# One PSUM pool, a fourth plain column tile, and a written order for pooling and attention in a two-layer trunk

## The chip, the cores and the metric

One core of a Trainium2 chip runs the whole model. The engines are TensorE (PE; its weight loads are listed as PEld), VectorE (DVE), ScalarE (ACT), GpSimd (POOL) and SyncE (SP). Time is device microseconds (us) of one execution; the kernel before took 1059.41 us as the median of 3 runs (1058.34 to 1059.82).

## The reference

A residual stream of 528 tokens (16 learned meta tokens, then 512) by 1024 features passes two layers and a final RMSNorm. Layer 0 mixes tokens by causal pooling, layer 1 by stick-breaking attention with 16 heads of 64; each is followed by a SwiGLU FFN with 2816 hidden features.

```python
h = concat(meta, x)                                       # (528, 1024)
h = h + pool_mixer(rmsnorm(h), pool_w, pool_scale)        # windows 2, 4, 8, 16
h = h + (silu(n @ w_gate[0]) * (n @ w_up[0])) @ w_down[0] # n = rmsnorm(h)
h = h + sb_attention(rmsnorm(h), w_qkv) @ w_o
h = h + (silu(n @ w_gate[1]) * (n @ w_up[1])) @ w_down[1]
out = rmsnorm(h)[16:]
# attention: z = q k / 8; a = exp(log_sigmoid(z) + sum over later allowed keys of log_sigmoid(-z)); o = a v
```

## The kernel before, in words

**Numbers.** Every operand of a large matmul is split into a high part (fp32r, by ACT: `whi`, `uh`, `hh`, `xh`) and the rest (by DVE: `wlo`, `ul`, `hl`, `xl`), and a product is three matmuls (high x high, high x low, low x high; `mm3`, L102). Weights come by DMA on SP's queue into a ring of 6 raw tiles and are split into rings of 8 (`wsplit`, L82; NW). Tiles of 128 x 528 share a ring of 29 (`blk`).

**FFN** (`ffn`, L269–476). The hidden features are 22 column tiles f of 128. The first PLAIN = 3 of them are made plainly: gate and up, 8 chunks of depth each (`plain`, L353). The others by one step of Strassen's scheme on pairs (`strassen`, L392): token halves, depth halves and the gate/up pair make seven products pa, pb, pc in place of eight. It needs sums of the weights (`sums`, L400) and of the normalised input (`operands`, L373: seven arrays `xh[i]`, `xl[i]` of 4 chunks, made once a layer in four rounds m of two chunks). The plain tiles use the input without the norm's factor and multiply by it after the product; so the norm's sum over features (a matmul with ones, `norm_bcast`, names `fb0`, `fb1`) is issued after the first gate product. ROUNDS cuts the 22 tiles into rounds; while a round's tiles are made, the previous round is multiplied by w_down (`down` in layer 0, over 264 tokens; `down_n` in layer 1, with tokens on partitions and 512 features, tiles `pd`).

**PSUM** has 8 banks. `phase` opens a pool for each part: the start with 8 single banks, FFN 0 with w = 6 and d = 2, attention with 4 single and 2 double tiles, FFN 1 with 6 and 2. A pool's banks are given to the next pool when everything in the old one is read.

**Start.** Pooling is matmuls of tokens (`ah`, `al`) with band matrices, two token halves for 8 chunks, scaled into `ph`, `pl`; then `mix`, per half and chunk, is added to the stream `hT`, and `norm.chunk` splits a chunk and sums its squares.

**Attention** (L486–723, in 8 pairs p of heads). For a pair: projections `pj` of q, k, v in five steps, scores `z` in three groups, sigmoids on ACT, a reverse scan on DVE (`kp`) and a product (`sg`), transposes `t`, products with v (`po`), and `wo`, the output projection of pairs 0–1, 2–4 and 5–7 (tiles `pw0_c`, `pw2_c`, `pw5_c` for chunk c), the first two of them placed between the pairs' steps.

**End.** In layer 1's last round each 128-token block t is finished by `square` (sum of squares on ACT) and `store` (factor, scaling, DMA out).

**Order.** A scheduler orders each engine's instructions by a simulated timeline; `tc.issue_after(x)` keeps what stands in it behind instruction x. The names' suffix in the profile leaves tile numbers out: pp is every plain product.

Of the kernel before, what the change touches and what calls it, by code (L numbers as in the profile page):

```python
# [13 lines left out]
P = 128  # L14
# [16 lines left out]
PLAIN = 3  # L31
# [19 lines left out]
def trunk(ctx: ExitStack, tc: tile.TileContext, x, meta, x_t, gain, pool_w, w_qkv, w_o, w_gate, w_up, w_down,  # L51
# [11 lines left out]
    @contextmanager  # L63
    def phase(name, **bufs):
        with tc.tile_pool(name=name, bufs=1, space=bass.MemoryType.PSUM) as pool:
            psum["pool"], psum["bufs"] = pool, bufs
            yield
# [33 lines left out]

    def mm3(outs, wh, wl, xh, xl, start, stop, more=False):  # L102

        for i, (w, xx) in enumerate(((wh, xh), (wh, xl), (wl, xh))):
            for o, sl in outs:
                last = nc.tensor.matmul(o, lhsT=w, rhs=xx[:, sl], start=start and i == 0, stop=stop and i == 2,  # L106
                                        skip_group_check=more)
        return last.ins
# [17 lines left out]
    def add_eps(out, sq, acc):  # L126

        nc.vector.scalar_tensor_tensor(out, sq, D * EPS / P, acc, op0=ALU.add, op1=ALU.add)

    last_rstd = []  # L130
# [11 lines left out]
    class Norm:  # L142
# [5 lines left out]
        def chunk(self, c):  # L148
# [9 lines left out]
            if c == KC - 1:  # L158
                add_eps(self.acc, sq, self.acc)
# [5 lines left out]
    def norm_bcast(accs, name, tag):  # L165
# [4 lines left out]
        for o in range(0, w, h):  # L170
            p = ps(f"{name}p{o}", tag)[:, :h]
            for i, acc in enumerate(accs):
                nc.tensor.matmul(p, lhsT=ones, rhs=acc[:, o:o + h], start=i == 0, stop=i == len(accs) - 1)
# [6 lines left out]
    with tc.tile_pool(name="start", bufs=1) as sp, phase("ps0", one=8):  # L180
# [52 lines left out]
        pw = ps("warm", "one")  # L233
# [3 lines left out]
        ph, pl = [], []  # L237
        for c in range(KC):
            for dst, n in ((ph, "ph"), (pl, "pl")):
                dst.append(blk(f"{n}{c}", F32R) if c < 6 else sp.tile([P, L], F32R, name=f"{n}{c}"))  # L240
        for hf, terms in enumerate((((0, -META), (1, -144)), ((1, 120), (2, HALF - 272), (3, -136)))):
            for c in range(KC):
                g = c // 2
                cs = slice(c * P, (c + 1) * P)
                pp = ps(f"pool{c}{hf}", "one")[:, :HALF]
                for j, (i, off) in enumerate(terms):
                    rhs = band[:, g, BOFF + off:BOFF + off + HALF]
                    nc.tensor.matmul(pp, lhsT=ah[i][:, cs], rhs=rhs, start=j == 0, stop=False)
                    nc.tensor.matmul(pp, lhsT=al[i][:, cs], rhs=rhs, start=False, stop=j == len(terms) - 1)
                    if hf == 0 and j == 0:  # L250
                        nc.tensor.matmul(pp[:, 0:32], lhsT=am[:, cs], rhs=mband[:, g, :], start=False, stop=False)
# [5 lines left out]
        for hf in range(2):  # L257
            for c in range(KC):
                g, d = c // 2, c % 2
                pm = ps(f"mix{c}{hf}", "one")[:, :HALF]  # L260
                for k in range(2):
                    ds = slice(d * P, (d + 1) * P)
                    mm3([(pm, HV[hf])], pws[k][0][g][:, ds], pws[k][1][g][:, ds], ph[2 * g + k], pl[2 * g + k],
                        k == 0, k == 1)
# [6 lines left out]
    def ffn(layer, gcol, norm, after):  # L271
# [48 lines left out]
        def down_n(r, t, e, hid, w, tag="d", sl=slice(0, 512)):  # L320
# [8 lines left out]
            for j, (wh, wl) in enumerate(zip(*w)):  # L329
                for i, (x_, w_) in enumerate(((0, wh), (1, wh), (0, wl))):  # L330
                    nc.tensor.matmul(pd, lhsT=hid[j][x_][:, ts], rhs=w_[:, sl], start=r > 0 and i + j == 0,  # L331
                                     stop=j == len(hid) - 1 and i == 2, skip_group_check=r == 0)
# [3 lines left out]
            else:  # L336
                nc.vector.tensor_tensor(out=hv, in0=pd, in1=hv, op=ALU.add)

        with tc.tile_pool(name=f"ffn{layer}", bufs=1) as fp:

            def wk(name):
                return fp.tile([P, HALF], F32, tag="wk", name=name, bufs=8)[:, :n]

            def gw(name):
                return fp.tile([P, L], F32, tag="gw", name=name, bufs=4)[:, :nt]
# [7 lines left out]
            def plain(f):  # L353
                parts = [wsplit(raw_gu(kind, f), f"w{kind}{f}") for kind in ("gate", "up")]
                g, sg, u = (gw(f"{i}{f}") for i in ("g", "sg", "u"))
                for dst, (wh, wl) in zip((g, u), parts):
# [444 lines left out]
```

## Time and profile before

| | |
|---|---|
| median of 3 runs | 1059.41 us (1058.34 to 1059.82) |
| the profiled execution | 1062.8 us |
| its span | 1061.0 us |
| granted PE clock, mean | 0.985 |
| PE busy | 1023.1 us, 96% |
| DVE busy | 856.6 us, 81% |
| ACT busy | 556.9 us, 52% |
| moved by DMA | 95.73 MB, mean 90 GB/s |

The span is cut here into the start (0 to 52), FFN 0 (52 to 403), attention (403 to 691) and FFN 1 (691 to 1061). A busy PE is the time in which its array is at work, at whatever clock the throttle granted; a stage with PE busy throughout and the clock at 1.00 runs at its cadence. The profile's rows give the time an instruction took alone; a run of equal ones is denser, since they overlap.

### The profile page before, as it was taken

Reading aid. Unit: us, or ns where it says so; the run is one execution under the profiler, and the core shown is the slowest. Engines: PE = TensorE matmul, PEld = TensorE weight load, DVE = VectorE, ACT = ScalarE, POOL = GpSimd, SP = SyncE. Lnnn points to the kernel's source line nnn. Section 1 sums busy time; section 2 is a strip of 40 time slices with the busy share of each in tenths; the row PEclk is TensorE's granted clock in tenths of the full one; section 3 lists DMA queues with packets and bytes.
Section 4 is the critical chain, followed back from the end, with each engine's and each line's share of the span. In section 5 each row is a group of like instructions: output and inputs, shape, how many; then the busy total and the mean of one; then the engine's idle time right before and its main releaser. Section 6 shows DMA issues by size and latency. Waiting matters only on the chain.

```text
span 1061.0 us, 18586 instructions
## 1 busy us (share of the span) xinstructions
PE 1023.1 (96%) x7302; PEld 949.3 (89%) x7302; DVE 856.6 (81%) x1529; ACT 556.9 (52%) x1131; POOL 6.2 (1%) x16
## 2 busy tenths in 40 slices
PE   8998999999999999999999998989999999999997
PEld 6997999999999998998888886867899999999985
DVE  7899987888878777678888987779977877788755
ACT  7555645454444455455555454555655444455544
POOL 1000000000000010000000000000000000000000
PEclk9999999999999999999999998989999999999999
DMA  9212323333333332211111211211223223333302
GB/s 351 72 51 69 128 94 100 101 100 100 100 100 100 99 120 82 78 40 61 40 51 37 69 58 66 80 62 58 100 100 115 84 100 99 100 100 120 109 31 80
DMA packets 43112, 95.73 MB, mean 90 GB/s; under 512 B 3328, under 2 KB 20096, under 8 KB 43024
## 3 DMA queue, kind: packets, MB, share of 16 engines
q1 hardware_dynamic: 42272, 93.40, 26.2%
q8 instruction: 57, 0.93, 0.3%
q10 hardware_dynamic: 752, 1.14, 0.3%
q14 instruction: 31, 0.25, 0.1%
HBM read 92.43 MB, written 2.10 MB: 89 GB/s over the span
## 4 chain that ended last, share of the span: by engine, by line
PE 78%; DVE 17%; issue 2%; ACT 1%; DMA 1%; SPq 0%; ACTq 0%; DVEq 0%
PE pb L106 15%; PE pd L106 11%; PE pd L331 11%; PE pa L106 10%; PE pc L106 10%; PE pj L106 9%; PE pp L106 4%; DVE kp L581 2%; PE pw L106 2%; PE z L567 2%; DVE xl L390 1%; DVE a L619 1%; PE t L594 1%; DVE t L387 1%; DVE sg L583 1%
## 5 line engine op out<-in xcount | busy, mean ns | idle before, releaser
L304 DVE TENSOR_TENSOR h<-pd,h 128x264 f32<-128x264 f32 x96 | 40.9, 427 | 14.0 <-PE pd L106 14.0
L92 ACT CAST ws_3h<-rgate 128x512 fp32r<-128x512 f32 x38 | 23.6, 620 | 53.3 <-PE pb L106 47.8
L581 DVE TENSOR_TENSOR_SCAN kp<-kp,estrip 128x1344 f32<-128x1344 f32 x16 | 47.3, 2954 | 3.8 <-ACT kp L576 3.4
L92 ACT CAST ws_4h<-s 128x512 fp32r<-128x512 f32 x38 | 23.6, 621 | 46.6 <-PE pa L106 27.7
L92 ACT CAST ws_5h<-s 128x512 fp32r<-128x512 f32 x38 | 23.6, 621 | 45.8 <-PE pb L106 34.7
L433 DVE TENSOR_TENSOR u<-pb,m 128x264 f32<-128x264 f32 (+1 forms) x38 | 16.3, 428 | 38.6 <-PE pb L106 38.6
L106 PE MATMUL pa<-xl,ws_0h 128*128 128x264 f32 (+1 forms) x152 | 43.3, 285 | 3.1 <-DVE xl L390 3.0
L106 PE MATMUL pb<-xl,ws_1h 128*128 128x264 f32 (+1 forms) x152 | 43.3, 285 | 1.0 <-DVE xl L390 1.0
L106 PE MATMUL pc<-xl,ws_2h 128*128 128x264 f32 (+1 forms) x152 | 43.1, 283 | 0.9 <-DVE xl L390 0.9
L106 PE MATMUL pb<-xh,ws_1h 128*128 128x264 f32 (+1 forms) x152 | 43.6, 287 | 0.2 <-ACT xh L389 0.2
L106 PE MATMUL pa<-xh,ws_3h 128*128 128x264 f32 (+1 forms) x152 | 43.6, 287 | 0.0
L106 PE MATMUL pa<-xl,ws_3h 128*128 128x264 f32 (+1 forms) x152 | 43.5, 286 | 0.0
L106 PE MATMUL pa<-xh,ws_3l 128*128 128x264 f32 (+1 forms) x152 | 43.3, 285 | 0.0
L106 PE MATMUL pc<-xh,ws_2l 128*128 128x264 f32 (+1 forms) x152 | 43.2, 284 | 0.0
L106 PE MATMUL pa<-xh,ws_0h 128*128 128x264 f32 (+1 forms) x152 | 43.1, 284 | 0.0
L106 PE MATMUL pb<-xh,ws_6l 128*128 128x264 f32 (+1 forms) x152 | 43.0, 283 | 0.0
L106 PE MATMUL pa<-xh,ws_0l 128*128 128x264 f32 (+1 forms) x152 | 43.0, 283 | 0.0
L106 PE MATMUL pb<-xh,ws_4l 128*128 128x264 f32 (+1 forms) x152 | 43.0, 283 | 0.0
L106 PE MATMUL pc<-xl,ws_5h 128*128 128x264 f32 (+1 forms) x152 | 42.9, 283 | 0.0
L106 PE MATMUL pb<-xh,ws_1l 128*128 128x264 f32 (+1 forms) x152 | 42.9, 283 | 0.0
L106 PE MATMUL pb<-xl,ws_4h 128*128 128x264 f32 (+1 forms) x152 | 42.9, 282 | 0.0
L106 PE MATMUL pc<-xh,ws_5h 128*128 128x264 f32 (+1 forms) x152 | 42.9, 282 | 0.0
(1179 smaller groups left out, 4110.9 us busy)
## 6 DMA issues: line engine op xcount, KB each, us to landing
rgate<-in_ffn_w_gate_dram SPq DMA_DIRECT2D x44, 512.0 KB, 3.5
rup<-in_ffn_w_up_dram SPq DMA_DIRECT2D x44, 512.0 KB, 3.5
rd<-in_ffn_w_down_dram SPq DMA_DIRECT2D x42, 512.0 KB, 3.6
rq<-in_sb_w_qkv_dram SPq DMA_DIRECT2D x8, 512.0 KB, 3.5
rk<-in_sb_w_qkv_dram SPq DMA_DIRECT2D x8, 512.0 KB, 3.4
rv<-in_sb_w_qkv_dram SPq DMA_DIRECT2D x8, 512.0 KB, 3.4
rwo<-in_sb_w_o_dram SPq DMA_DIRECT2D x8, 384.0 KB, 3.0
h<-in_x_t_dram SPq DMA_DIRECT2D x8, 264.0 KB, 6.9
```

Of the source, the lines that this page charges most:

```text
L92: nc.scalar.copy(hi, v[:, j:j + w])
L106: last = nc.tensor.matmul(o, lhsT=w, rhs=xx[:, sl], start=start and i == 0, stop=stop and i == 2, skip_group_check=more)
L304: nc.vector.tensor_tensor(out=hv, in0=pd, in1=hv, op=ALU.add)
L331: nc.tensor.matmul(pd, lhsT=hid[j][x_][:, ts], rhs=w_[:, sl], start=r > 0 and i + j == 0, stop=j == len(hid) - 1 and i == 2, skip_group_ch ...
L387: nc.vector.tensor_tensor(out=o, in0=a, in1=b, op=ALU.subtract)
L390: nc.vector.tensor_tensor(out=xl[i][:, m, :], in0=o, in1=f32(xh[i][:, m, :]), op=ALU.subtract)
L433: tt(out=u[:, a], in0=pb, in1=m1, op=ALU.add)
L567: nc.tensor.matmul(tz[:, hd, c:c + k1 - k0], lhsT=qq[hs, i * P:(i + 1) * P], rhs=kk[hs, k0:k1], start=j == 0 and c == 0, stop=False, skip_ ...
L581: nc.vector.tensor_tensor_scan(kp[:, hd, ::-1], kp[:, hd, ::-1], estrip[:, ::-1], 1.0, op0=ALU.mult, op1=ALU.max)
L583: return nc.vector.tensor_tensor(out=sg[:, hd, 0:STRIP - 1], in0=sg[:, hd, 0:STRIP - 1], in1=kp[:, hd, 1:STRIP], op=ALU.mult).ins
L594: nc.tensor.transpose(o, sg[:, c0:c0 + n], ident)
L619: nc.vector.scalar_tensor_tensor(a0[r, i], f32(a0h[r]), lo_rows[r], p2[r, 256:384], op0=ALU.mult, op1=ALU.add)
```

## The change

- PLAIN is 4: tile f = 3 of each layer is made plainly.
- One PSUM pool for the whole program, with tags `two` (2 tiles of two banks), `c` and `d` (2 of one bank each). `one` takes c and d in turn, `any` in the start goes round all eight banks, `ps_pair` gives a plain tile's two accumulators as a two-bank tile or as two of c. Strassen's pa and pb share a two-bank tile, `pab`.
- Pooling is issued in the written order, each chunk behind the one before; `mix` follows all pooling and goes chunk by chunk with both halves together.
- In the first plain tile the norm's matmul is issued inside the up product, behind its depth chunk FB = 4; both products are scaled and moved out after. The split of the plain tiles' weights stands behind the norm's last sum, or behind its factor for the later ones.
- `operands` works in two rounds of four chunks, with arrays of double width.
- In attention `queued` makes a chain of PE's steps as written, in `begin`, `turned`, `attend` and the projections.
- In the last round of layer 1 two products of the round before are held back (LATE = 2) until behind the last Strassen product, then the last products follow by token block, each behind the one before. The last block's store is cut into two halves of 256.
- Silu is written over its input, `wk` tiles come in pairs, `gw` has 3 buffers for 4.

```diff
-PLAIN = 3
+PLAIN = 4
+LATE = 2
+FB = 4
...
-    def phase(name, **bufs):
-        with tc.tile_pool(name=name, bufs=1, space=bass.MemoryType.PSUM) as pool:
+    psum = ctx.enter_context(tc.tile_pool(name="psum", bufs=1, space=bass.MemoryType.PSUM))
+    turn = {"one": 0, "any": 0, "pair": 0}
     def ps(name, tag, banks=1):
+        i = turn.get(tag, 0)
+        turn[tag] = i + 1
+        if tag == "any":
+            if i % 8 in (0, 1, 4, 5):
+                if i % 2 == 0:
+                    turn["tile"] = ps(name, "two", 2)
+                return turn["tile"][:, i % 2]
+            tag = "cd"[i % 2]
+        if tag == "one":
+            tag = "cd"[i % 2]
         shape = [P, 512] if banks == 1 else [P, banks, 512]
-        return psum["pool"].tile(shape, F32, tag=tag, name=name, bufs=psum["bufs"][tag])
+        return psum.tile(shape, F32, tag=tag, name=name, bufs=2)
+    def ps_pair(name):
+        i = turn["pair"]
+        turn["pair"] = i + 1
+        if i % 3 == 2:
+            return [ps(f"{name}{j}", "c") for j in range(2)]
+        pt = ps(name, "two", 2)
+        return [pt[:, 0], pt[:, 1]]
...
-                pp = ps(f"pool{c}{hf}", "one")[:, :HALF]
+                pp = ps(f"pool{c}{hf}", "any")[:, :HALF]
+                with tc.issue_after(pooled.ins) if pooled else nullcontext():
...
-        for hf in range(2):
-            for c in range(KC):
+        for c in range(KC):
+            for hf in range(2):
...
             def plain(f):
-                parts = [wsplit(raw_gu(kind, f), f"w{kind}{f}") for kind in ("gate", "up")]
+                for kind in ("gate", "up"):
+                    with tc.issue_after(norm.done if f <= 2 - layer else fst[1]) if f else nullcontext():
+                        parts.append(wsplit(raw_gu(kind, f), f"w{kind}{f}"))
...
-                    if not fst:
-                        fst.extend((norm_bcast([acc], f"fb{layer}", "d"), last_rstd[0]))
+                        if i == 1 and k == FB and not fst:
+                            with tc.issue_after(last):
+                                fst.extend((norm_bcast([acc], f"fb{layer}", "d"), last_rstd[0]))
+                            mark = last_bcast[0]
...
-                for m in range(4):
+                for m in (0, 2):
...
-                        t = fp.tile([P, L], F32, tag="xn", name=f"xn{c}", bufs=2)
+                        t = fp.tile([P, 2, L], F32, tag="xn", name=f"xn{c}", bufs=2)
...
-                pa, pb, pc = [ps(f"p{i}{f}", "w")[:, :n] for i in "abc"]
+                pab = ps(f"pab{f}", "two", 2)
+                pa, pb, pc = pab[:, 0, :n], pab[:, 1, :n], ps(f"pc{f}", "c")[:, :n]
...
-                                down_n(r - 1, t, e, prev, w)
+                                rest.append(lambda r=r, t=t, e=e, prev=prev, w=w: down_n(r - 1, t, e, prev, w))
+                            while len(rest) > (LATE if r == len(ROUNDS) - 1 else 0):
+                                rest.pop(0)()
...
+            for st in rest:
+                with tc.issue_after(prods_end[0]):
+                    st()
...
-                    square(t, e, sl, hvs[e], box)
+                    with tc.issue_after(mark) if mark else nullcontext():
+                        mark = down_n(r, t, e, prev, ws[e], "dc"[e], sl)
+                    square(t, e, sl, hvs[e], box)
...
+        def queued(*steps):
+            for st in steps:
+                with queue():
+                    pos[:] = [st()]
...
+            queued(*before, lambda: (sc.group(0), sc.group(1))[1], *between, lambda: sc.group(2))
...
+            w = 512 if t < 3 else 256
+            cuts = [slice(o, o + w) for o in range(0, 512, w)]
```

What moves on the engines, at three places. In each fence a row is an instruction as it stands in the program, output <- inputs and size; a line of "..." leaves rows out.

PE in attention's last pair, p = 7, before: `pw2_c` is the output projection of pairs 2–4, chunk c (nine matmuls each), `z7_416` the last group of the last pair's scores, `po61` the product with v of pair 6's second head.

```order
L106 MATMUL pw2_1_8125<-os4h_7538,wo2_1l0_8122 128x512
L106 MATMUL pw2_2_8163<-os2h_6830,wo2_2h0_8159 128x512
...
L106 MATMUL pw2_3_8178<-os2h_6830,wo2_3h0_8174 128x512
...
L567 MATMUL z7_416_8136<-qk7_1h_7787,qk7_0h_7849 128x400 x2
...
L573 MATMUL z7_416_8136<-masks_63 128x128
L106 MATMUL pw2_3_8178<-os3h_7158,wo2_3h0_8174 128x512
...
L633 MATMUL po61_8189<-a161h_8058,vv6_7645 128x512
```

And in the change:

```order
L129 MATMUL pw2_1_7962<-os4h_7375,wo2_1l0_7959 128x512
L616 MATMUL z7_416_7973<-qk7_1h_7624,qk7_0h_7686 128x400 x2
...
L622 MATMUL z7_416_7973<-masks_66 128x128
L129 MATMUL pw2_2_8000<-os2h_6667,wo2_2h0_7996 128x512
...
L129 MATMUL pw2_3_8015<-os2h_6667,wo2_3h0_8011 128x512
...
L129 MATMUL pw2_3_8015<-os4h_7375,wo2_3l0_8012 128x512
L694 MATMUL po61_8026<-a161h_7895,vv6_7482 128x512
```

The last group of scores stood behind pw2_2 and three matmuls of pw2_3; it now stands right behind pw2_1, twelve matmuls earlier.

PE at the start of FFN 1, before: `pw5_7` is the last matmul group of attention, `pp0` the products of the first plain tile (gate and up), `fb1` the norm's matmul.

```order
L106 MATMUL pw5_7_8528<-os7h_8359,wo5_7l0_8525 128x512
L106 MATMUL pp0_8591<-f1uh0_8380,wgate0h0_8570 128x512
L106 MATMUL pp0_8591<-f1ul0_8381,wgate0h0_8570 128x512
...
L106 MATMUL pp0_8591<-f1uh5_8493,wgate0h4_8574 128x512
L106 MATMUL pp0_8629<-f1uh0_8380,wup0h0_8580 128x512
...
L106 MATMUL pp0_8591<-f1uh7_8539,wgate0l4_8575 128x512
...
L173 MATMUL fb1p0_8616<-f1sq0_8384,ones_62 128x264
L173 MATMUL fb1p264_8618<-f1sq0_8384,ones_62 128x264
L106 MATMUL pp0_8629<-f1uh3_8447,wup0h0_8580 128x512
```

And in the change, where `pp00` is the gate product, `pp01` the up product, `pp1` and `pp2` the next two plain tiles:

```order
L129 MATMUL pw5_7_8365<-os7h_8196,wo5_7l0_8362 128x512
L129 MATMUL pp1_8571<-f1uh0_8217,wgate1h0_8551 128x512
L129 MATMUL pp1_8571<-f1ul0_8218,wgate1h0_8551 128x512
L129 MATMUL pp00_8423<-f1uh0_8217,wgate0h0_8403 128x512
...
L129 MATMUL pp00_8423<-f1uh5_8330,wgate0h4_8407 128x512
L129 MATMUL pp2_8650<-f1uh0_8217,wgate2h0_8630 128x512
...
L129 MATMUL pp00_8423<-f1uh7_8376,wgate0l4_8408 128x512
L129 MATMUL pp01_8424<-f1uh0_8217,wup0h0_8413 128x512
...
L197 MATMUL fb1p0_8464<-f1sq0_8221,ones_65 128x264
```

The first two matmuls of pp1 and of pp2 come ahead, the gate product is whole before the up product begins, and the norm's matmul stands behind 43 matmuls that follow pw5_7 rather than 33.

DVE in FFN 0 at the first round of `operands`, before: `xn` is the normalised chunk, `t` a sum, `xl` a low part.

```order
L381 SCALAR_TENSOR_TENSOR xn0_709<-h0_66,gains_64,fb0r_641 128x528
L381 SCALAR_TENSOR_TENSOR xn4_711<-h4_70,gains_64,fb0r_641 128x528
...
L387 TENSOR_TENSOR t0_713<-xn0_709 128x264
...
L390 TENSOR_TENSOR xl0_557<-xn0_709,xh0_550 128x264
...
L390 TENSOR_TENSOR xl3_560<-xn4_711,xh3_553 128x264
L390 TENSOR_TENSOR xl5_562<-xn4_711,xh5_555 128x264
```

And in the change:

```order
L423 SCALAR_TENSOR_TENSOR xn0_694<-h0_69,gains_67,fb0r_658 128x528
L423 SCALAR_TENSOR_TENSOR xn0_694<-h1_70,gains_67,fb0r_658 128x528
L423 SCALAR_TENSOR_TENSOR xn4_697<-h4_73,gains_67,fb0r_658 128x528
L423 SCALAR_TENSOR_TENSOR xn4_697<-h5_74,gains_67,fb0r_658 128x528
...
L429 TENSOR_TENSOR t0_700<-xn0_694 128x528
L433 TENSOR_TENSOR xl0_545<-xn0_694,xh0_538 128x528
...
L433 TENSOR_TENSOR xl3_548<-xn4_697,xh3_541 128x528
L433 TENSOR_TENSOR xl5_550<-xn4_697,xh5_543 128x528
```

Each round makes four normalised chunks, not two, and sums and low parts of 528 columns, not 264; there are two rounds, not four.

More of the change, by code (lines that the diff above doesn't have):

```diff
@@ L107, in mm3 @@
                                         skip_group_check=more)
+        last_mm[:] = [last.ins]
         return last.ins
@@ L158, in chunk @@
             if c == KC - 1:
-                add_eps(self.acc, sq, self.acc)
+                self.done = add_eps(self.acc, sq, self.acc)
             elif c:
@@ L179, in trunk @@
     norm = Norm(16, "f0")
-    with tc.tile_pool(name="start", bufs=1) as sp, phase("ps0", one=8):
+    with tc.tile_pool(name="start", bufs=1) as sp:
         nc.scalar.activation(sp.tile([P, 1], F32, name="table"), ones[:, 0:1], AF.Abs_reciprocal_sqrt)
@@ L232, in trunk @@
         nc.vector.memset(warm, 0.0)
-        pw = ps("warm", "one")
+        pw = ps("warm", "d")
         for _ in range(WARM):
@@ L256, in trunk @@
         pws = [wsplit(pwr[k], f"pw{k}") for k in range(2)]
-        for hf in range(2):
-            for c in range(KC):
+        for c in range(KC):
+            for hf in range(2):
                 g, d = c // 2, c % 2
[L260 to L264, printed above, removed]
+                pm = ps(f"mix{c}{hf}", "any")[:, :HALF]
+                with tc.issue_after(pooled.ins):
+                    for k in range(2):
+                        ds = slice(d * P, (d + 1) * P)
+                        mm3([(pm, HV[hf])], pws[k][0][g][:, ds], pws[k][1][g][:, ds], ph[2 * g + k], pl[2 * g + k],
+                            k == 0, k == 1)
                 hv = hT[c][:, HV[hf]]
@@ L330, in down_n @@
                 for i, (x_, w_) in enumerate(((0, wh), (1, wh), (0, wl))):
-                    nc.tensor.matmul(pd, lhsT=hid[j][x_][:, ts], rhs=w_[:, sl], start=r > 0 and i + j == 0,
-                                     stop=j == len(hid) - 1 and i == 2, skip_group_check=r == 0)
+                    last = nc.tensor.matmul(pd, lhsT=hid[j][x_][:, ts], rhs=w_[:, sl], start=r > 0 and i + j == 0,
+                                            stop=j == len(hid) - 1 and i == 2, skip_group_check=r == 0)
             hv = hn[4 * e + t][:, sl]
@@ L480, in before_attention @@
         return norms[0].chunk
-    with phase("ps1", w=6, d=2):
-        ffn(0, 16, norm, before_attention)
-    with tc.tile_pool(name="att", bufs=1) as ap, phase("ps2", one=4, two=2):
+    ffn(0, 16, norm, before_attention)
+    with tc.tile_pool(name="att", bufs=1) as ap:
         uh, ul, acc = norms[0].uh, norms[0].ul, norms[0].acc
@@ L668, in begin @@
             sc = Scores(p, got["q"], got["k"])
-            mark = None
-            for st in before:
-                mark = st()
-            with tc.issue_after(mark) if mark else nullcontext():
-                sc.group(0)
-                mark = sc.group(1)
-            for st in between:
-                with tc.issue_after(mark):
-                    mark = st()
-            with tc.issue_after(mark):
-                sc.group(2)
+            queued(*before, lambda: (sc.group(0), sc.group(1))[1], *between, lambda: sc.group(2))
             sc.both()
@@ L686, in trunk @@
         sg = begin(0, got, [], steps[3:4])
-        steps[4]()
+        queued(steps[4])
         values()
         nxt, steps, values = proj(1)
-        for st in steps[:3]:
-            st()
+        queued(*steps[:3])
         early, w = wo(0, 2), wo(2, 5)
@@ L696, in trunk @@
             w0 = turned(p, 0, sg[:, 0])
-            for st in steps[3:] if p + 1 < NP else w[4:6]:
-                st()
+            queued(*(steps[3:] if p + 1 < NP else w[4:6]))
             if p + 1 < NP:
                 values()
-            attend(p, 0, w0, v, of)
+            queued(lambda: attend(p, 0, w0, v, of))
             w1 = turned(p, 1, sg[:, 1])
```

129 lines of the change are left out of this document (72 added, 57 removed).

## The prediction

> **What bounds the kernel now.** I read the page first, then the busy time by stage, then PE's waits, then PE's timeline at each place where it idles.
>
> ```profile
> span 1061.0 us, 18586 instructions
> PE 1023.1 (96%) x7302; PEld 949.3 (89%) x7302; DVE 856.6 (81%) x1529; ACT 556.9 (52%) x1131; POOL 6.2 (1%) x16
> PE 78%; DVE 17%; issue 2%; ACT 1%; DMA 1%; SPq 0%; ACTq 0%; DVEq 0%
> ```
>
> PE sets the end, and 17% of the chain of waits is DVE: there PE stands and DVE works. Where that is, the stages tell (the columns are the stretch, its length, busy time of PE, its weight loads, DVE, ACT and POOL with instruction counts, the granted clock, the DMA share, GB/s):
>
> ```profile
> core 0: us, PE busy (x) PEld busy (x) DVE busy (x) ACT busy (x) POOL busy (x), PEclk, DMA share, GB/s
> 38.80:52.50 13.70, 13.44 (x95) 13.34 (x96) 11.09 (x18) 7.37 (x13) 0.00 (x0) 0.88 0.23 79
> 79.50:97.00 17.50, 13.05 (x76) 10.93 (x75) 17.50 (x44) 8.52 (x22) 0.00 (x0) 0.90 0.13 46
> 97.00:400.00 303.00, 303.00 (x2490) 303.00 (x2490) 247.19 (x467) 155.29 (x314) 3.27 (x10) 1.00 0.32 105
> 400.00:431.00 31.00, 28.69 (x201) 25.86 (x201) 18.57 (x33) 17.36 (x26) 0.00 (x0) 0.94 0.20 72
> 653.00:690.60 37.60, 34.01 (x153) 28.15 (x153) 31.42 (x47) 18.17 (x39) 0.00 (x0) 0.91 0.21 71
> 690.60:702.00 11.40, 7.25 (x20) 5.49 (x19) 11.02 (x18) 5.48 (x9) 0.00 (x0) 0.70 0.27 92
> 738.00:753.00 15.00, 12.42 (x70) 10.56 (x69) 15.00 (x36) 10.92 (x28) 0.00 (x0) 0.89 0.10 36
> 753.00:1049.00 296.00, 296.00 (x2045) 275.08 (x2044) 226.98 (x414) 149.34 (x309) 0.00 (x0) 1.00 0.28 93
> ```
>
> The two long FFN stretches (97–400, 753–1049) have no PE idle at full clock: nothing that the change does there on DVE or ACT can be worth time, only a change in PE's work. In the short stages PE idles with DVE full (79.5–97 and 738–753: 17.50 of 17.50 and 15.00 of 15.00), and the granted clock falls below 1. That fall comes in steps; here it is in consecutive stretches of 3.41 us, about the length at which the clock changes:
>
> ```profile
> 653.25:656.67 3.42, 0.61 (x4) 0.29 (x3) 3.42 (x4) 0.58 (x1) 0.00 (x0) 1.00 0.00 0
> 656.67:660.08 3.41, 2.63 (x12) 2.56 (x13) 3.41 (x2) 1.23 (x5) 0.00 (x0) 0.50 0.45 154
> 660.08:663.50 3.42, 3.42 (x10) 2.64 (x9) 3.36 (x4) 1.22 (x3) 0.00 (x0) 0.50 0.00 0
> ```
>
> PE idles for most of the first and then gets half the clock for the next two. So a stall costs itself and up to two such stretches at half speed, about 1.7 us of matmul work each.
>
> **The change part by part.** Cadences of matmuls, from the chain of waits in the steady stretches:
>
> ```profile
> 168.75 1.83 PE pd L106 x15
> 823.12 3.72 PE pd L331 x16
> 813.70 2.84 PE pb L106 x24
> ```
>
> That is 0.122 us for 264 columns, 0.2325 for 512, 0.118 for 256.
>
> *Fourth plain tile.* A plain tile has 96 matmuls of 264 columns in layer 0 where Strassen's has 84, so +12 x 0.122 = +1.5 us; in layer 1 48 x 0.2325 - 84 x 0.118 = 11.2 - 9.9 = +1.2 us. Against it stand the stalls at the first Strassen tile. In 79.5–97 76 matmuls ran, 9.3 us at 0.122, so 8.2 us went lost (8.5 when I walk the starts one by one). In 738–753 the idle is 2.6 us and the lower clock costs 0.11 x 15 = 1.7, at least 4.3; walked start by start against the cadence of each shape it is 5.9. What PE waits for is the lower half of the operands:
>
> ```profile
> PE pp L106 <- DVE h L660: 4.1, 1, 4.1
> PE t L594 <- DVE sg L583: 3.6, 1, 3.6
> PE pa L106 <- DVE xl L390: 3.0, 3, 2.1
> PE z L567 <- ACT qk_1h L527: 1.6, 1, 1.6
> ```
>
> The fourth plain tile gives DVE another 96 x 0.122 = 11.7 us in which PE has work, and the operands get cheaper: two rounds of double width instead of four.
>
> ```profile
> L390 DVE TENSOR_TENSOR xl<-t,xh 128x264 fp32r<-128x264 f32 x13 | 5.2, 421 | 0.0
> L367 DVE TENSOR_TENSOR u<-sg,u 128x528 f32<-128x528 f32 x3 | 2.1, 697 | 0.0
> ```
>
> Of 44 such instructions of 0.42 us, 22 of 0.70 remain: 18.5 - 15.4 = 3.1 us less on DVE. In its new order DVE also has the third tile's two evacuations, product and split before the last operand. Adding DVE's row durations in that order from the norm's end, I get the last operand (xl6) at about 93 us, and PE needs it at about 97, after three plain tiles, the first down products and six Strassen products. The margin is 4 us of some 41 summed, so I leave 1.0 us of stall: 8.5 - 1.0 - 1.5 = 6.0 gained (between -1.5, nothing saved and the work paid, and 7.0). In layer 1 the same walk ends at 749, needed at 751: 5.9 - 0.5 - 1.2 = 4.2 gained (-1.2 to 4.7).
>
> *One PSUM pool.* At the second FFN's start PE waits for the end of the attention's pool:
>
> ```profile
> 690.62 0.40 PE L106 MATMUL pw<-os7h,wo_7l 128*128 128x512 f32 x1
> 695.16 0.77 PE L106 MATMUL pp<-f1uh,wgate0h 128*128 128x512 f32 x1 [4.15 <-DVE h L660]
> ```
>
> pp's first operands and weights are ready before 690.6, but its banks are freed only by the last evacuation h at 695.0. In the change pp's banks belong to earlier, finished users, so pp starts right behind pw5_7. 20 matmuls in these 11.4 us would be 4.65 at full clock; with the wait, the two stretches at half clock and the two norm matmuls 7.5 us were lost. What is late next is the last norm chunk: h of chunk 7 on DVE after 691, then its split. With the splits of the second and third tiles' weights moved behind the sums of squares (L118 behind norm.done), DVE has it by about 694, and the order gives PE 25 matmuls (5.8 us, to 696.8) before it is needed. I take 7.0 (3.3, if the chunk is 2 us late and one half-clock stretch comes back, to 7.5). The two products' evacuation moves behind both; covered by pp1, whose matmuls follow.
>
> At the attention's start (400–431) the same border goes, but PE there waits for the chain chunk 7, rstd, q, k (qk_1h in the waits above), which stays as it is: 0.5 (-1.5 to 3.6).
>
> *Attention's order.* Up to the last pair PE's order is the old one, so it costs nothing. In the last pair z7_416 moves ahead of twelve matmuls:
>
> ```profile
> 649.63 0.46 PE L567 MATMUL z<-qk_1h,qk_0h 64*128 64x400 f32 x4
> 653.47 0.39 PE L633 MATMUL po<-a,vv 128*128 128x512 f32 x1
> 657.45 2.36 PE L594 MATMUL t<-consts,sg 128*128 128x128 f32 x10 [3.59 <-DVE sg L583]
> 668.41 0.40 PE L106 MATMUL pw<-os2h,wo_6h 128*128 128x512 f32 x1
> 651.83 2.96 DVE L581 TENSOR_TENSOR_SCAN kp<-kp,estrip 128x1344 f32<-128x1344 f32 x1 [1.64 <-ACT kp L576]
> 655.76 1.55 DVE L583 TENSOR_TENSOR sg<-sg,kp 128x1343 f32<-128x1343 f32 x1
> ```
>
> 12 x 0.2325 = 2.8 us earlier: z at 646.8, scan at 649.0, h and a split, sg at 653.0, transposes at 654.6; PE has pw2_2, pw2_3 and po61 until 653.7, so it waits 0.9 instead of 3.6. Late next is po70: the second scan, h, a split, of6 and sg come before a170l, which is ready at about 661.6, where PE arrives at 659.9; then 0.65 for a. pw2_6 starts at 664.8 instead of 668.41: 3.6 without a clock drop, 1.9 with one. I take 2.8.
>
> The clock decides between these two. A stretch need not be empty (the columns now: length, busy time of PE, granted clock, DMA share, GB/s):
>
> ```profile
> 421.16:424.57 3.41, 1.79 (x14) 1.00 0.13 35
> 424.57:427.98 3.41, 3.41 (x23) 0.50 0.31 124
> ```
>
> PE was busy 1.79 of 3.41 us, and the next stretch ran at half clock. The Trainium skill ("TensorE: Matmul & The Clock Gate", Part 1, What's actually happening) says that the array goes cold after at least one idle window of about 3.4 us; this trace shows it with half a window of work. By the page's rule the new idles of 0.9, 1.7 and 0.65 us would cost no clock and the sum below would come to 1037.1; I go by the row.
>
> *Start.* Pooling in written order waits for al1, then the second half needs pl0 and pl1, so PE idles some 3 us near 17–20. DVE's norm chain sets the start's end: pooling ends 2 us later, but mix now goes chunk by chunk and the first norm chunk comes earlier. The norm's matmul inside the up product comes when the sum is done. I add 0 (-2 to +3 us of gain, what 38.8–52.5 loses to its clock of 0.88 and more).
>
> *End.* After the last matmul (1053.06) the span runs 8 us:
>
> ```profile
> 1053.00 1.52 ACT fsq L738 x6
> 1056.57 0.72 ACT hn L748
> ```
>
> Here token block 2's square and store still stand on ACT between block 3's. With blocks in order, 0.6 of the 1.52 us of squares goes, and the last hn is cut into halves of about 0.4: 1.0 (0 to 1.6). LATE and the queue of last products move only PE work that had no gap; the 24 late products (5.6 us) cover the last tile's silu and split. The shared wk, gw and xn tiles save DVE and ACT instructions beside a full PE: 0.
>
> Sum: 6.0 + 4.2 + 7.0 + 0.5 + 2.8 + 0 + 1.0 = 21.5 us. The profiled execution took 1062.8 itself (span 1061.0, 1.8 around it), 3.4 above the median of the runs, so it would be 1041.3, and the runs 1059.4 - 21.5 = **1037.9**.
>
> **Rivals.**
> - *DVE still gates the Strassen operands.* DVE is full in both stages, my margin is 4 and 2 us, and weight splits of the new first tile wait for slots of a ring of 8 that the first down products hold. Then neither stall goes and PE pays 2.7 us: 0.5 + 2.8 + 7.0 + 1.0 - 2.7 = 8.6, so 1050.8. Against it: the 11.7 us of new cover exceed the 8.5 lost.
> - *The clock comes back down.* New idles at pooling, at the attention's ends and at the first FFN each bring a half-clock stretch: three more of 1.7 us, 1043. The rows at 421–428 speak for it; against it, each stands before work that is DVE-bound anyway or is short.
> - *All goes.* Every stall above falls to its bound (7.0 + 4.7 + 7.5 + 3.6 + 1.6 and 3 + 2 at start and attention's start): 1030.
> - *Slower: the two-bank tile is held as one.* Strassen's first two accumulators pa and pb now lie in one tile. If the program makes PE wait for the copy of one half before it writes the other, products two and five stand some 0.42 us each (ACT's 264-wide copies take 0.41 beside DVE's 0.42) in all 36 Strassen tiles: +30 us, and with 21.5 gained 1068. It decides once the wait exceeds 21.5 / 36 = 0.6 us a tile. Against it: the halves are separate banks, and the ring is two tiles deep as before.
>
> ```profile
> L389 ACT CAST xh<-t 128x264 fp32r<-128x264 f32 x16 | 6.3, 409 | 3.2 <-DVE t L387 3.2
> ```
>
> **How the numbers follow.** Forecast 0.65 (1032 to 1044), DVE still gating 0.15, the clock 0.08, all gone 0.07, slower 0.05. The predicted time is the forecast's 1038. The range goes from the case in which all goes, 1030, to the first rival's 1051. A measurement of this kernel can tell about 0.2%, 2.1 us, from no change. Slower by more: 0.05. Within: 0.03, the upper end of the first rival with the second. Faster: 0.92.
>
> **What would show it.** Right: pp begins within 0.5 us of pw5_7's end and no clock below 1 follows; no PE wait on xl above 1 us; the transposes of pair 7 wait under 1.2 us for sg; PE's long stretches keep full busy time at clock 1.00; the span ends some 6.5 to 7 us after the last matmul. Wrong: PE waits for xl or for ACT's ws splits at the first Strassen tile; PE waits for ACT's copies inside the steady Strassen tiles; the norm of the second FFN holds pp at its sixth chunk; the start's first pp1 matmul comes more than 2 us after 52.5.

## The result, and the profile after

The changed kernel took 1054.58 us (median of 5 runs, 1052.04 to 1056.65) against 1059.82 for the kernel before (5 runs, 1058.34 to 1062.61): a ratio of 0.9946, 95% interval 0.9926 to 0.9966. It is 5.2 us faster; 21.5 were forecast, and the time lies outside the range of 1030 to 1051. Its profiled execution took 1055.18, 0.6 above its median; the one of before stood 3.0 above its own, so between the profiles (spans 1061.0 and 1053.4) the difference looks larger, 7.6 us. Of the experiments below, e2_free and e10_last_tile had one execution each, the profiled one, at a mean clock of 0.74 and 0.85 (1252.84 and 1097.99 us); neither its trace nor its time is used.

The page of the changed kernel:

```profile
span 1053.4 us, 18429 instructions
PE 1021.6 (97%) x7278; PEld 946.7 (90%) x7278; DVE 846.3 (80%) x1468; ACT 545.2 (52%) x1088; POOL 7.3 (1%) x16
PE 84%; DVE 11%; issue 2%; ACT 2%; DMA 1%; SPq 0%; ACTq 0%; DVEq 0%
```

DVE's share of the chain fell from 17% to 11%: much of what was to go did go. The busy time by stage shows what came in its place (columns as in the prediction):

```profile
core 0: us, PE busy (x) PEld busy (x) DVE busy (x) ACT busy (x) POOL busy (x), PEclk, DMA share, GB/s
10.50:38.80 28.30, 21.02 (x118) 19.39 (x119) 18.49 (x35) 15.33 (x29) 0.00 (x0) 0.76 0.64 240
60.00:97.00 37.00, 37.00 (x304) 36.90 (x303) 35.99 (x68) 19.17 (x35) 0.00 (x0) 1.00 0.25 80
700.00:711.00 11.00, 11.00 (x49) 8.92 (x48) 8.50 (x15) 5.20 (x10) 0.00 (x0) 1.00 0.30 97
711.00:760.00 49.00, 49.00 (x261) 41.68 (x260) 48.10 (x81) 28.60 (x51) 0.00 (x0) 1.00 0.28 90
760.00:1043.00 283.00, 282.13 (x1925) 260.88 (x1924) 219.32 (x396) 144.04 (x297) 0.00 (x0) 1.00 0.29 95
```

The same first stretch of the kernel before:

```profile
10.50:38.80 28.30, 24.69 (x192) 23.60 (x192) 26.30 (x53) 20.76 (x41) 0.00 (x0) 1.00 0.67 244
```

The stretches where the first Strassen tiles stood (60–97, 711–760) and the start of the second FFN (700–711) are full now, at clock 1.00. The start is not: 118 matmuls where there were 192, and a clock of 0.76. PE's waits in the whole execution, the three longest:

```profile
PE pool L275 <- DVE pl L282: 6.3, 4, 2.6
PE pw L129 <- DVE of L697: 2.1, 2, 1.1
PE z L616 <- ACT qk_1h L576: 1.7, 1, 1.7
```

Four waits for `pl`, the scaled low part of a pooled chunk. In PE's timeline they are these:

```profile
12.80 0.39 PE L276 MATMUL pool<-band,al 128*128 128x264 f32 x1
15.75 0.59 PE L275 MATMUL pool<-band,ah 128*128 128x264 f32 x1 [2.56 <-DVE pl L282]
...
22.85 0.59 PE L275 MATMUL pool<-band,ah 128*128 128x264 f32 x1 [1.51 <-DVE pl L282]
...
29.56 0.39 PE L275 MATMUL pool<-band,ah 128*128 128x264 f32 x1 [1.10 <-DVE pl L282]
...
33.86 0.39 PE L275 MATMUL pool<-band,ah 128*128 128x264 f32 x1 [1.10 <-DVE pl L282]
```

The matmul at 15.75 is the first one of chunk 1. Chunk 0 was complete at 13.2; ACT and DVE read it here:

```profile
14.11 0.47 ACT L281 ACTIVATE ph<-pool,gains 128x264 fp32r<-128x264 f32 x1
15.21 0.49 DVE L282 SCALAR_TENSOR_TENSOR pl<-pool,gains,ph 128x264 fp32r<-128x264 f32 x1
```

Both come late because ACT and DVE split the weights of mix until 14.2 and 15.2. Chunk 1 fills the second bank of the tile whose first bank holds chunk 0, and it starts when the reading of chunk 0 ends. The other three stand at chunk 5 and at chunks 1 and 5 of the second token half: each time the second half of a two-bank tile. The program's own order shows it before any run. These are the last matmul of chunk 0, which waits for al, and the first two of chunk 1, of which the first waits for DVE though its operands are long there; the count of DVE's semaphore that it waits for is the one that `pl` of chunk 0 raises:

```
L276 MATMUL pool_207<-band,al_118 128x264 [waits DVE_49]
L275 MATMUL pool_207<-band,ah_113 128x264 [waits DVE_49]
L276 MATMUL pool_207<-band,al_117 128x264
```

The idle brings the clock down, here in stretches of 3.41 us (columns: length, PE busy, clock, DMA share, GB/s):

```profile
11.33:14.74 3.41, 1.39 (x5) 1.00 1.07 382
14.74:18.15 3.41, 2.40 (x11) 0.50 1.08 383
18.15:21.57 3.42, 3.20 (x14) 0.50 1.02 400
21.57:24.98 3.41, 2.13 (x10) 0.50 1.04 412
24.98:28.39 3.41, 3.41 (x16) 0.50 0.85 318
28.39:31.80 3.41, 2.31 (x19) 1.00 0.02 5
```

Four stretches at half clock. So the last pooling matmul moved from 24.9 to 36.0 us and the first norm matmul from 51.4 to 59.7, though it now stands behind more matmuls. Between start and end the lines that the prediction names read so, at the second FFN's start and in the last pair of heads:

```profile
694.89 0.39 PE L129 MATMUL pw<-os7h,wo_7l 128*128 128x512 f32 x1
695.12 0.40 PE L129 MATMUL pp<-f1uh,wgate1h 128*128 128x512 f32 x1
```

```profile
660.62 1.28 PE L654 MATMUL t<-consts,sg 128*128 128x128 f32 x10 [0.83 <-DVE sg L632]
667.88 0.49 PE L694 MATMUL po<-a170l,vv 128*128 128x512 f32 x1 [1.31 <-DVE a170l L677]
```

### The profile page after: what moved, and what is told of

Read it like the earlier page. It is cut to its first block, busy times and chain, and to the rows that moved or that the text cites. A ratio compares the mean times of both kernels' runs of the same rounds, so it can differ in the third digit from the quotient of the medians.

```text
span 1053.4 us, 18429 instructions
## 1 busy us (share of the span) xinstructions
PE 1021.6 (97%) x7278; PEld 946.7 (90%) x7278; DVE 846.3 (80%) x1468; ACT 545.2 (52%) x1088; POOL 7.3 (1%) x16
## 4 chain that ended last, share of the span: by engine, by line
PE 84%; DVE 11%; issue 2%; ACT 2%; DMA 1%; SPq 0%; ACTq 0%; DVEq 0%
PE pab L129 25%; PE pd L129 12%; PE pd L359 12%; PE pc L129 10%; PE pj L129 9%; PE pp L129 8%; PE pw L129 3%; DVE kp L630 2%; PE z L616 2%; DVE a L680 1%; DVE sg L632 1%; PE t L654 1%; PE mix L129 1%; PE pool L275 1%; DVE of L697 1%
## 5 line engine op out<-in xcount | busy, mean ns | idle before, releaser
L129 PE MATMUL pab<-xh,ws_6h 128*128 128x264 f32 (+1 forms) x144 | 40.7, 283 | 0.9 <-ACT mb L464 0.9
L129 PE MATMUL pab<-xh,ws_1h 128*128 128x264 f32 (+1 forms) x144 | 40.7, 283 | 0.2 <-ACT ma L457 0.2
L129 PE MATMUL pab<-xh,ws_6l 128*128 128x264 f32 (+1 forms) x144 | 40.8, 283 | 0.0
L129 PE MATMUL pab<-xh,ws_0l 128*128 128x264 f32 (+1 forms) x144 | 40.8, 283 | 0.0
L129 PE MATMUL pab<-xh,ws_4l 128*128 128x264 f32 (+1 forms) x144 | 40.8, 283 | 0.0
L129 PE MATMUL pab<-xl,ws_1h 128*128 128x264 f32 (+1 forms) x144 | 40.7, 283 | 0.0
L129 PE MATMUL pab<-xl,ws_3h 128*128 128x264 f32 (+1 forms) x144 | 40.7, 283 | 0.0
L129 PE MATMUL pab<-xl,ws_6h 128*128 128x264 f32 (+1 forms) x144 | 40.7, 282 | 0.0
L129 PE MATMUL pab<-xh,ws_3l 128*128 128x264 f32 (+1 forms) x144 | 40.7, 282 | 0.0
L129 PE MATMUL pab<-xh,ws_1l 128*128 128x264 f32 (+1 forms) x144 | 40.6, 282 | 0.0
```

## The experiments

Theory: a two-bank PSUM tile is held as one, so where its two halves are filled and read one after the other, the second waits for the first's reading; together with the written order, which lets nothing else pass, this costs the start what it was thought to cost nowhere. Rival: the written order itself is the loss. Then each other gain is tried by undoing one part.

**Both halves filled before either is read.** The edit in pooling:

```diff
-            for c in range(KC):
+            for c0 in range(0, KC, 2):
+                pps = []
+                for c in (c0, c0 + 1):
...
+                    pps.append((c, pp))
...
+                for c, pp in pps:
+                    gc = gains[:, c:c + 1]
...
```

> The changed kernel, but in pooling the matmuls of two chunks are issued first and both are read after, so a two-bank tile is full before its first half is read; the written order and the one pool stay. Theory 'held as one': in the changed kernel the four second halves (chunks 1 and 5 of each token half) wait for the reading of the first half (6.3 us of waits on pl, and with the restarts and the half clock that follows some 8 to 10 us). They go; pooling's last matmul moves from 36.0 to about 27, the first norm matmul from 59.7 to about 51, the time from 1054.6 to about 1046. Rival 'written order': the order itself makes PE wait for al1, al2 and the evacuations; then the waits move to other chunks and the time stays at 1054 +- 2.

Measured: 1046.0 (ratio to before 0.9866, 0.9850 to 0.9883). The last pooling matmul is at 29.0, the first norm matmul at 53.3. The time is the one that the theory gives, though pooling and norm come some 2 us later than expected; the written order is still there.

**The same in mix** (both token halves of a chunk multiplied, then both added).

> As e1_pairs, and mix's two halves of a chunk are also both multiplied before both are added. Theory 'held as one': mix shares two-bank tiles in the same way, so a further 0 to 2 us: 1044 to 1046; mix was seen with only 0.4 us of waits. Rival 'written order': 1054 +- 2, like the changed kernel.

Measured: 1044.24 (0.9852, 0.9833 to 0.9872); not told apart from the kernel above, but not slower. Its start:

```profile
PE pool L278 <- DVE pl L286: 1.8, 1, 1.8
PE pool L279 <- DVE al L251: 1.4, 2, 0.7
```

One wait on pl is left, for a tile of the ring that was not yet read. This kernel is the base of what follows, called the pairs kernel.

**No written order, halves filled in pairs:** the two issue_after of pooling and mix are left out of the pairs kernel.

```diff
-                with tc.issue_after(pooled.ins) if pooled else nullcontext():
+                with nullcontext():
...
-                with tc.issue_after(pooled.ins):
+                with nullcontext():
```

> The kernel e1b_pairs_mix without the written order of pooling and mix. If the order has a price of its own beyond the shared tiles (0.85 + 1.96 us of waits at 19 to 24 and the half clock after), pooling ends near the 25 us of the kernel before and the first norm matmul comes 2 to 4 us earlier: 1041. If DVE's chain sets the end of the start, no change: 1044.

Measured: 1043.63 (0.9849, 0.9831 to 0.9867), the first norm matmul at 51.0 against 50.7. The order by itself costs nothing that can be measured.

**No written order, halves read singly:** the same edit on the changed kernel.

> The changed kernel without the written order of pooling and mix, each half of a two-bank tile read as soon as it is full (as in the changed kernel). With e8_pool_free (1043.6, both halves filled first, free order) and the changed kernel (1054.6) it splits the loss at the start: if sharing alone costs it, the second halves still come after the reading of the first and 1050 to 1054 remains; if it takes the written order too, so that nothing else can fill the wait, the free order puts other chunks there and the time is 1044 to 1047.

Measured: 1047.74 as the median of the other three runs (0.9881, 0.9857 to 0.9905). It was profiled once more:

> The kernel e2_free once more, for an undisturbed profile. If sharing costs time by itself, PE still has one or two waits on pl at a second half (1 to 2.5 us each) and pooling ends 2 to 5 us later than the 30.5 us of e8_pool_free; the time is 1047 to 1048. If the free order covers the waits, pooling ends within 1 us of it and the 4 us between the two kernels lie elsewhere.

1047.62 (0.9883, 0.9862 to 0.9903). Waits of its start, and for comparison of the kernel with free order and pairs:

```profile
PE pool L275 <- DVE pl L282: 3.2, 2, 2.7
```

```profile
PE pool L278 <- DVE pl L286: 3.3, 1, 3.3
```

The sums of the waits are alike; pooling ends at 34.1 instead of 30.5 and the first norm matmul comes at 55.5 instead of 51.0. So the four kernels make a square:

| | halves in pairs | halves singly |
|---|---|---|
| free order | 1043.6 | 1047.7 |
| written order | 1044.2 | 1054.6 (the change) |

(In the singly read kernels mix is read singly too.) Sharing costs some 4 us alone, the order 0.6 (within its noise), both together 11 (10 by the ratios to the kernel before). The rival falls; the order matters only because it leaves nothing to put into the wait. The 4 us between the two kernels of free order are not in the waits on `pl`. More than half is in the clock: the singly read one has three stretches of 3.41 us at half clock in its start (18.54 to 25.37 and 49.27 to 52.68), which lose 4.2 us against the matmuls' cadence, the other has one (19.86 to 23.27), which loses 1.4. Whether these stretches come from the sharing is not shown.

**Plain tiles.** PLAIN = 4 alone on the kernel before:

> The kernel before with a fourth plain tile and nothing else (operands still in four narrow rounds, old pools and orders). If the plain tile alone covers the operands, both stalls at the first Strassen tile go (8.5 and 5.9 us) and PE's work grows by 2.7: 1059.8 - 11.7 = 1048. If the narrow operands still gate it, half of the stalls stay: about 1054. If the stalls only move, 1062.

Measured: 1053.48 (0.9931, 0.9906 to 0.9955), near the second number. The trace of its profiled run, which took 1048.85, shows no wait on xl over 0.2 us; what is left at the first Strassen tile of layer 0 is

```profile
PE pd L106 <- ACT hh L349: 1.0, 1, 1.0
PE pb L106 <- ACT xh L389: 0.6, 1, 0.6
```

and nothing in layer 1. The plain tile alone covers the operands' low parts; against the cadence 2.3 of the 8.5 us remain in layer 0, so by the trace 6.2 + 5.9 - 2.7 = 9.4 us are gained. The other runs, 1052.8 to 1054.4, are slower than the profiled one at a lower mean clock, 0.988 to 0.990 against 0.994. One stretch of 3.41 us at half clock lowers the mean by 0.0016, so by estimate they have two to four such stretches more; where these lie no trace shows.

PLAIN = 3 in the changed kernel:

> The changed kernel with three plain tiles. If the fourth plain tile is what removed the Strassen stalls, they come back, less some 3 us of cheaper operands in each layer, and PE's work falls by 2.7: 1054.6 + 5.5 + 3 - 2.7 = about 1060. If the operands of double width alone removed them, the time falls to 1052.

Measured: 1066.46 (1.0062, 1.0046 to 1.0077), 11.9 above the change and more than I expected. Layer 0 and layer 1:

```profile
PE pc L129 <- DVE xl L433: 2.5, 1, 2.5
PE pab L129 <- DVE xl L433: 1.6, 1, 1.6
```

```profile
PE pd L359 <- DVE hl L379: 2.6, 1, 2.6
PE pab L129 <- DVE xl L433: 2.5, 1, 2.5
```

With three tiles the double width removes neither stall: counted start by start against the cadence, 8.0 and 9.2 us are lost where the kernel before lost 8.5 and 5.9. In layer 1 the FFN's start loses 7 us less than before, so PE is earlier at this tile, which fits the longer stall: part of the other gain goes there. Most of the gain at the two places is thus the fourth plain tile's; narrow operands in the changed kernel were not run, so what the double width adds to it is open. The two stalls, 17.2 us, less 2.7 of work would give 14.5. The whole is 11.9, since attention loses 3.5 less in this trace: it has no stretch at half clock there, the change's has two.

**PSUM border.** The pairs kernel, with a second, equal pool for the second FFN:

```diff
+    first.close()
+    pools[0] = ctx.enter_context(tc.tile_pool(name="psum2", bufs=1, space=bass.MemoryType.PSUM))
     ffn(1, 24, norms[1], final)
```

> The kernel e1b_pairs_mix, with its PSUM pool closed at attention's end and an equal one opened for the second FFN. If the pool border is what held the second FFN's first product, PE again waits some 4 us for the last evacuation and gets two stretches at half clock: +7, about 1051. If the norm's chain would have held it anyway, +1 at most, 1045.

Measured: 1047.46 (0.9880, 0.9858 to 0.9901), 3.2 more, between the two. The intervals still touch, but the trace has the loss in one place, 2.6 us between the last projection and the norm's matmul:

```profile
688.02 0.47 PE L130 MATMUL pp<-f1uh,wgate0h 128*128 128x512 f32 x1 [2.34 <-DVE h L728]
```

The border is a wait of 2.3 us, not of 4.15, and no half clock follows. In the kernel before DVE had splits of the next tiles' weights ahead of the last evacuation, which ended 4.4 us after the start of the last projection matmul; without them it ends 2.6 us after.

**Splits behind the norm.** The pairs kernel with the plain tiles' splits free (`issue_after(norm.done ...)` left out):

> The kernel e1b_pairs_mix, with the plain tiles' weight splits free to go ahead of the norm's last sum. The pool border alone was worth 3 of the 7 us that the second FFN's start gained. If the rest came from DVE's order (splits behind the norm's sums), DVE is late again with the last chunks: 2 to 4 us more in the starts of the two FFNs, 1046 to 1048. If not, no change, 1044.

Measured: 1050.12 (0.9911, 0.9884 to 0.9939), 5.9 more. The loss is not at the second FFN's start, where pp still begins at once, and not ahead of the norm's matmuls: layer 0's comes at 55.9 instead of 50.7 because 46 more matmuls stand in front of it. It lies behind them, where later tiles wait for the late evacuation (g), in layer 0 and in layer 1:

```profile
PE pp L129 <- DVE g L411: 2.2, 1, 2.2
```

```profile
PE pc L129 <- DVE g L411: 1.6, 1, 1.6
```

Behind each wait comes a stretch at half clock (61.69 to 65.11 and 740.94 to 744.36), so each layer loses some 4 us against the cadence. Attention loses 3.2 us less in this trace, without a stretch at half clock where the pairs kernel's trace has two.

**Norm's matmul earlier,** FB = 0 for 4 in the pairs kernel:

> The kernel e1b_pairs_mix, with the norm's matmul behind the first depth chunk of the up product instead of the fifth (12 or 24 matmuls earlier, 2.8 us). If the place inside the up product matters, PE now waits for the norm's last sum: 2 to 3 us more in each FFN start, 1047 to 1050. If the sum is ready anyway by then, no change and the factor comes earlier: 1044.

Measured: 1047.06 (0.9878, 0.9855 to 0.9901), 2.8 more, with intervals that overlap. PE waits for the norm's last sum in both layers; this is layer 0's, the other is 0.8:

```profile
PE fb0p L197 <- DVE f0sq L152: 0.7, 1, 0.7
```

So FB = 0 is too early by these waits, 1.5 us. The rest is not shown to be the edit's: in this trace pooling, which the edit leaves as it is, already ends at 30.2 instead of 28.6. Other places were not run.

**Attention's chain** left out of the pairs kernel (scores as in the kernel before):

```diff
-            return tc.issue_after(pos[0]) if pos else nullcontext()
+            return nullcontext()
```

> The kernel e1b_pairs_mix without the chain of PE steps in attention (scores as in the kernel before, all else in the scheduler's order). The last pair's z7_416 stands right behind pw2_1 also without the chain, so the scan is as early; but projections pw2_4 and pw2_6 now stand in front of the transposes and among the products po70. If the chain made PE wait in the last pair (0.99 + 1.47 + 0.51 us, and the half clock after it), those waits go: 3 to 5 us less, about 1040. If the chain was needed, the waits of the kernel before return: 1046 to 1048.

Measured: 1051.1 (0.9918, 0.9900 to 0.9937), 6.9 more, against my expectation. The waits in attention:

```profile
PE t L660 <- DVE sg L638: 7.7, 4, 2.6
PE pw L129 <- DVE of L703: 3.0, 2, 2.3
```

Without the chain the scheduler puts transposes where they wait for sg at four places; in the kernel before, which has no chain, the only such wait was the last pair's. So the chain gains nothing over the kernel before but is needed in this one; that it is the one pool which changes the scheduler's order, and none of the other parts, is not shown. That z7_416 stood behind pw2_1 in this kernel too shows that its early place does not come from the chain.

**End of the last round.** The pairs kernel with the two held-back products free:

```diff
-                with tc.issue_after(prods_end[0]):
-                    st()
+                st()
```

> The kernel e1b_pairs_mix, with the two products that are held back (LATE) free to stand among the last Strassen products. The changed kernel has one wait of 1.02 us there, for the copy of the fifth product, with nothing between the fifth and the seventh. If the queue causes it, it goes: 1.0 less, 1043; too little for the times, so the trace decides (wait at the last tile's seventh product). If not, no change.

Measured: 1048.66 (0.9896, 0.9874 to 0.9918), 4.4 more, against my expectation. The wait of 1.0 goes and a larger one comes, since nothing is left to cover the last tile's silu and split:

```profile
PE pd L365 <- ACT hh L384: 3.1, 1, 3.1
```

The last tile's sixth product kept behind its fifth:

```diff
-                prod(pc, ws4, 5, False)
+                with tc.issue_after(last_mm[0]) if f == ROUNDS[-1][1] - 1 and layer else nullcontext():
+                    prod(pc, ws4, 5, False)
```

> The kernel e1b_pairs_mix, with the last Strassen tile's sixth product kept behind its fifth, so that PE has 12 matmuls (1.4 us) while ACT copies the fifth. The wait of 1.02 us at the seventh product goes: 1.0 less, 1043; the trace decides.

Measured: 1044.43 as the median of the other three runs (0.9852, 0.9825 to 0.9879), no change; profiled once more:

> The kernel e10_last_tile once more, for an undisturbed profile. In the disturbed one a wait of 1.02 us stood at the fifth product instead of the seventh. If the wait only moves to the next product without work between, the same stands here and the end is unchanged; if the disturbance made it, no wait over 0.5 us stands in the last tile and the last matmul comes 1.0 us earlier, counted from the second FFN's start.

1046.81 in one run. The wait has only moved, to the fourth product:

```profile
1003.51 0.28 PE L129 MATMUL pab<-xh,ws_1l 128*128 128x256 f32 x1
1004.65 0.39 PE L129 MATMUL pab<-xh,ws_3h 128*128 128x256 f32 x1 [0.86 <-ACT ma L465]
```

The row at 1004.65 is a product into the half pa; what it waits for, line 465 of that kernel, is the copy of the other half, pb, into m6. pa's own copy was done long before. So the tile is held as one in Strassen's tiles too; elsewhere other products stand between and cover it. The wait in the changed kernel and in the pairs kernel is another one: there the seventh product (`ws_6`) waits for the copy of the fifth into m67, and both are products into pb, so this wait would stand with a tile for each half too.

```profile
1017.21 0.38 PE L129 MATMUL pab<-xh,ws_6h 128*128 128x256 f32 x1 [0.86 <-ACT mb L464]
```

## Why the prediction was wrong, point by point

The size of each step by the profiles, counted from matmul start to matmul start against the cadence of its shape:

| step | forecast gain | found |
|---|---|---|
| first Strassen tile, layer 0 | 6.0 | 8.5 lost before, 0 after, +1.5 of work: 7.0 |
| first Strassen tile, layer 1 | 4.2 | 5.9 lost, 0 after, +1.2: 4.7 |
| second FFN's start | 7.0 | 7.5 lost before, 0.4 after: 7.1 |
| attention's start | 0.5 | 3.7 lost before, 5.8 after: -2.1 |
| attention's end | 2.8 | 6.8 lost before, 5.1 after, from the last score to the last projection: 1.7 |
| start | 0 | 9.9 lost before, 18.7 after: -8.8 |
| last tile, held-back products | 0 | a wait of 1.0 that was not there: -1.0 |
| end behind the last matmul | 1.0 | 8.24 before, 6.89 after: 1.35 |

The rows add up to 10.0 us, the profiles differ by 7.6. The larger part of the rest is in attention: from 380 us to the last projection 24.0 us were lost before and 25.5 after, 1.5 more where the two rows have 0.4 more. No row of attention is surer than some 3 us: the pairs kernel and the one without written order have PE's matmuls there in the same sequence and lost 25.1 and 22.2, the first with two stretches at half clock, the second with none.

- **The step that failed is the start**, "I add 0 (-2 to +3 us of gain)". I let the second token half wait for pl0 and pl1 and looked no further; that chunk 1 waits for the reading of chunk 0, since they share a tile, I did not see. The reason given, that DVE's norm chain sets the start's end, fell with it: pooling was 11 us late, mix 12, and DVE's chain waited for them. Taking the sharing's wait away gives back 8.6 us, and in the pairs kernel the start up to the first norm matmul loses 8.2 us where the kernel before lost 8.1: without the sharing the 0 would have been right. The start is 8.8 of the 13.9 us by which the profiles miss the 21.5.
- **The mechanism was among the rivals, at the wrong place.** "The two-bank tile is held as one" was priced for Strassen's tiles and dismissed because "the halves are separate banks". Held as one is what the program does, in both places. In the changed kernel's Strassen tiles it cost next to nothing, where 30 us were priced: in the steady stretches, 97 to 400 and 711 to 1043 us, PE's only wait of 0.4 us or more for a copy of theirs is that of 0.9 us at the end, which is not the sharing's; in pooling, where the halves are used one after the other in a written order, it decided.
- **The fourth plain tile** did what was said in the trace, and removing it costs 11.9. The argument with the operands' double width is not borne out: with three tiles the stall is about as long as before in layer 0 and longer in layer 1. On the kernel before the fourth tile gave 6.0 in the timed runs, of 9.4 by the trace.
- **One pool**: the second FFN's start is right in size (7.1), wrong in its share: the border alone is 2.3 to 3.2 us; the rest goes with DVE's splits in front of the last evacuation, and with the clock that falls behind it. In the pairs kernel with free splits that evacuation again ends 4.4 us after the start of the last projection matmul, as in the kernel before, and PE does not wait for it, so the one pool covers both parts. Undoing the splits' place costs 5.9, undoing the norm's matmul's 1.5 by its waits.
- **Attention**: the waits in the last pair came as walked, 0.83 for sg (0.9 forecast) and 1.31 for a170l (1.7). z7_416's early place is not the chain's doing. What the forecast left out is the start of attention: PE waits twice for the last chunks' low parts (anul, 1.5 us together). DVE has a split there ahead of the last low part, but so it had before (wq's, now wk's). New is PE's order: the first projections stand among the last down products (from 394.0, before from 408.8), which leaves PE less to do at the wait. The clock falls behind it as it did before.
- **The rival of the clock** came true in one of its places and as the consequence of the start's waits: four half-clock stretches in the start, where the kernel before had one. Attention has two, where it had three, and the second FFN's start none, where it had two. The price of a stall, itself "and up to two such stretches", was read too low: here it was four.
- **The range** ended at 1051 because it was cut at the first rival's centre and had no case of the start's loss, though its bound "-2" was worked out from no row at all. At the other end the case "all goes" took 2 at attention's start, whose own bound is 3.6; by the bounds it gives 1028, which changes nothing here.

The best kernel of this study is the pairs kernel, with or without the written order: 1044.2 and 1043.6, 1.5% below before (ratios 0.9852 and 0.9849) and some 10 us below the change. By the profiles the pairs kernel gains 16.9 of the 21.5 us. What is missing is attention, which loses 1.2 more than before where 3.3 were to be gained, and the last tile's wait of 1.0; the start is not among it. Of attention's 4.5, some 3 are within what the clock alone changes there between two traces.

## What to carry to other kernels

Where two accumulations share a tile, look in the program's order for a wait of the second on the reader of the first; fill both before reading either. A tile for each, as in the kernel before, should do the same; that was not run. A written order cost nothing here once nothing in it had to wait for the shared tile, and made each such wait dear (11 us against 4). A term put at zero needs a row for its bound as much as the large ones do.

## What the runs showed of the hardware

The clock drops after less idle than a whole stretch: in the rows from 11.33 on, a stretch with 1.39 of 3.41 us busy is followed by four at 0.50, though PE was busy 3.20 of 3.42 in the second of them. It came back there after a stretch without any idle (24.98 to 28.39). That is no rule of these traces. In the start of the kernel with FB = 0 two full stretches were followed by another at 0.50:

```profile
12.84:16.25 3.41, 3.41 (x16) 0.50 1.05 390
16.25:19.67 3.42, 3.42 (x18) 0.50 1.07 385
19.67:23.08 3.41, 3.41 (x17) 0.50 1.03 412
23.08:26.49 3.41, 2.90 (x24) 1.00 0.86 338
```

In the kernel before, a half-clock stretch with 3.16 of 3.41 us busy (86.65 to 90.06) was the last. Nor do the traces give a bound for the fall: 1.79 busy (kernel before, 421.16 to 424.57) brought the clock down, 1.78 (its copy with four plain tiles, 414.28 to 417.69) did not. The Trainium skill ("TensorE: Matmul & The Clock Gate", Part 1, What's actually happening) has the array warm again after one busy window and cold after one idle one; the first agrees with the row at 24.98 and not with those at 12.84 and 16.25, the second does not agree with the row at 11.33.
